# Logsumexp of a Strassen-like matmul: two row tiles by DMA transpose and last, first loads uncast, four blocks with B's sums stationary

## The chip, the cores and the metric

The kernel runs on one core of a Trainium2 chip. The metric is the device time of one execution in microseconds; lower is better. TensorE (PE) multiplies, VectorE (DVE), ScalarE (ACT) and GpSimd (POOL) do the elementwise work, GpSimd and SyncE (SP) issue the DMAs.

## The reference

```python
def setup_inputs():
    m, k, n = 1024, 4096, 4096
    return {"a": np.random.randn(m, k).astype(np.float32),
            "b": np.random.randn(k, n).astype(np.float32)}

def reference(a, b):
    x = np.matmul(a, b)
    return special.logsumexp(x, axis=-1).astype(np.float32)
```

One number per row of A: the logarithm of the sum of the exponentials of that row of A times B.

## The kernel before

Everything is multiplied in f16 and summed in f32. A has 8 row tiles of 128 rows, K has 32 tiles of 128, and B is cut into 8 column blocks of 512. A program order written by hand fixes the order of each engine.

**Stage 1, block 0.** A and B arrive by DMAs that GpSimd issues and that cast f32 to f16 on the way. A's row tiles 0 to 5 come in 8 rounds of 4 K tiles, with the matching pieces of B's block 0 between them; row tiles 6 and 7 follow in pieces of 8 K tiles. TensorE transposes each 128x128 piece of A (`transpose_group`, L194) into PSUM; VectorE and ScalarE copy it in turns to `aT`. Behind that, `plain` (L212) multiplies each transposed piece by 512 columns of block 0: 256 products of 512 columns. Six row tiles hold six PSUM banks, two banks serve the transposes; tiles 6 and 7 take banks that tiles 0 and 1 gave back. `tb` serves as staging space for the pieces of A in this stage (12 slots) and holds B's sums later.

**Blocks 1 to 7.** Each pair of row tiles (a quad q, 0 to 3), each pair of K tiles (i, 0 to 15) and the two halves of 256 columns form a 2x2 product, done with 7 products in place of 8 (a Strassen-Winograd-like scheme). It needs sums of A's parts (`s1`, `s2`, `s5` and two made in place in `aT`; `a_sums_early`, `a_sums_late`) and sums of B's parts for each block (`T1`, `T4`, `T6` in `tb`, and two made in place, called t7 and t3). `m1` to `m7` each issue 16 matmuls of 256 columns through `product` (L357), with A's side stationary (128x128, loaded anew for each matmul) and B's side moving: 7 x 16 x 4 = 448 per block. ScalarE copies parts out (`e`, `s`), VectorE puts the quad's four results together, takes each row's maximum (`lse_max`, L86), and ScalarE does the exponential with its sum (`lse_exp`, L91). In quad 3 of a block VectorE also makes the next block's sums. B's blocks are loaded one block ahead, four DMAs of 1 MB (f16) each (L130), into 8 buffers (`bt_pool`): a buffer is free once the block before has been multiplied. In block 1 the first two quads are worked on together, one quarter of K at a time.

**The end.** In the last quad of block 7 the seventh product goes to a bank of its own, `z`. While it runs, `combine` merges the maxima and sums of the eight blocks per row, and the last row tile's two halves are merged apart. Then one small DMA stores the result.

Of the kernel before, what the change touches and what calls it, by code (L numbers as in the profile page):

```python
# [13 lines left out]
def kernel(  # L14
# [21 lines left out]
    SC = 1024  # L36
    KC, JT = K // SC, SC // P
    G = 4
    GI = KP // G
    assert (MT, KT, NB) == (8, 32, 8) and JT == 2 * GI and KC == G  # L40

    a_m = a.rearrange("(p mt) k -> mt p k", mt=MT)

    cst_pool = ctx.enter_context(tc.tile_pool(name="cst", bufs=1))
    bt_pool = ctx.enter_context(tc.tile_pool(name="btp", bufs=2 * G))
    fix_pool = ctx.enter_context(tc.tile_pool(name="fix", bufs=1))
    psum_pool = ctx.enter_context(
# [20 lines left out]
    T1, T4, T6 = tb[:, 0], tb[:, 1], tb[:, 2]  # L68
    stg_slots = tb.rearrange("p t (i j) n -> p (t i) (j n)", j=4)
    NSLOT = 3 * KP // 4  # L70
    ident = cst_pool.tile([P, P], f16, name="ident")
# [40 lines left out]
    def combine(m0, m1, n, ln=True, between=None):  # L112
        nm, dd = nmmin[:, m0:m1], d[:, m0:m1, 0:n]
        nc.vector.tensor_reduce(out=nm, in_=negmax[:, m0:m1, 0:n], axis=AX.X, op=ALU.min)
        sub(dd, negmax[:, m0:m1, 0:n], nm.unsqueeze(-1).broadcast_to((P, m1 - m0, n)))
        nc.scalar.activation(out=dd, in_=dd, func=AF.Exp, scale=-1.0)
        if between:
            between()
        nc.vector.tensor_mul(out=dd, in0=dd, in1=tsum[:, m0:m1, 0:n])
        nc.vector.tensor_reduce(out=lg[:, m0:m1], in_=dd, axis=AX.X, op=ALU.add)  # L120
        if ln:
            nc.scalar.activation(out=lg[:, m0:m1], in_=lg[:, m0:m1], func=AF.Ln)

    def load_b(nb, g, parts=1):
        bt = bt_pool.tile([P, GI, 2, FD], f16, name=f"b_{nb}_{g}", tag="bt")
        step = 2 * GI // parts
        flat = bt.rearrange("p i t n -> p (i t) n")
        rows = b.rearrange("(k p) n -> p k n", p=P)
        for h in range(parts):
            nc.gpsimd.dma_start(  # L130
                out=flat[:, h * step : (h + 1) * step],
                in_=rows[:, g * 2 * GI + h * step : g * 2 * GI + (h + 1) * step, ts(nb, FD)],
            )
        return bt

    class Block:
        def __init__(self, nb):
            self.nb, self.raw = nb, []
# [4 lines left out]
        def rawg(self, g, kp, h):  # L143
            return self.raw[g][:, :, kp, ts(h, H)]

        def do_t1(self, g):
            add(T1[:, ts(g, GI)], self.rawg(g, 0, 0), self.rawg(g, 1, 1))

        def do_t4(self, g):
            sub(T4[:, ts(g, GI)], self.rawg(g, 1, 0), self.rawg(g, 0, 0))  # L150

        def do_t6(self, g):
            add(T6[:, ts(g, GI)], self.rawg(g, 0, 0), self.rawg(g, 0, 1))

        def do_t7(self, g):
            add(self.rawg(g, 1, 0), self.rawg(g, 1, 0), self.rawg(g, 1, 1))

        def do_t3(self, g):
            sub(self.rawg(g, 0, 1), self.rawg(g, 0, 1), self.rawg(g, 1, 1))
# [4 lines left out]
    blk0 = Block(0)  # L164
# [74 lines left out]
    rounds = []  # L239
    for kn in (4,) * 8:  # L240
        k0 = sum(rounds)
        rounds.append(kn)
        for m in range(MT - 2):
            arrivals.append((k0, kn, "a", m))
            if m < kn // 2:
# [8 lines left out]
    def behind(k0, kn, what, x):  # L254
# [6 lines left out]
        for k, m in todo:  # L261
            if m == MT - 2 and k == 0:
                acc.append(acc_tiles("l"))
            plain(acc[m // 2][m % 2], k // 2, k % 2, m)
        r = slice(k0 // 2, (k0 + kn) // 2)
        if what == "a" and x < MT - 2:
            if x >= 3 and len(in_place) >= 3:
                a_sums_late(*in_place.pop(0))
            if x % 2 == 1:
# [3 lines left out]
        if what == "a" and k0 + kn == KT and x in (4, 5):  # L273
            first_max(2 * x - 8)
            first_max(2 * x - 7)
        if what == "a" and x >= MT - 2:
            n = 2 * (k0 // JT) + x - (MT - 2)
            if n < 2:
                first_max(4 + n)
            elif in_place:  # L280
                a_sums_late(*in_place.pop(0))
# [7 lines left out]
    warm(10)  # L289
    blk = Block(1)  # L290

    def load(k0, kn, what, x):
        if what == "a":
            load_a(k0, kn, x)
            return
        if k0 % JT == 0:
            blk0.raw.append(bt_pool.tile([P, GI, 2, FD], f16, name=f"b_0_{k0}", tag="bt"))
        nc.gpsimd.dma_start(
            out=blk0.raw[k0 // JT][:, k0 % JT // 2],
            in_=b[k0 * P : (k0 + 2) * P, ts(0, FD)].rearrange("(t p) n -> p t n", p=P),  # L300
        )

    coming = list(arrivals)
    back = []
    for n, (k0, kn, what, x) in enumerate(arrivals):
        while coming and (coming[0][2] == "b" or loads[0] < count[0] + NSLOT):
            load(*coming.pop(0))
            if len(coming) == len(arrivals) - 3:
                make_identity(nc, ident)
                nc.gpsimd.memset(negmax, 3.0e38)  # L310
                nc.gpsimd.memset(tsum, 0.0)
        if not coming and not blk.raw:
            for g in range(G):
                blk.raw.append(load_b(1, g))
        if what == "a":
            transpose_group(k0, kn, x)
        if k0 < rounds[0] and x < 3:
            warm(1)
        if len(back) == min(3, 1 + n // 8):
            behind(*back.pop(0))  # L320
        back.append((k0, kn, what, x))
    while back:
        behind(*back.pop(0))

    for g in range(G):
        if g == 2:
            for m in range(MT - 2, MT):
                first_max(m)
        for f in (blk.do_t1, blk.do_t6, blk.do_t4, blk.do_t7, blk.do_t3):
            f(g)  # L330

    pending = []

# [5 lines left out]
    for nb in range(1, NB):  # L339
        nxt = None  # L340
        if nb + 1 < NB:
            nxt = Block(nb + 1)
            for g in range(G):
                nxt.raw.append(load_b(nb + 1, g))
        quads = {}
        for q in range(MP):
            if q not in quads:
                both = (0, 1) if nb == 1 and q == 0 else (q,)
                for p in both:
                    quads[p] = acc_tiles(f"{nb}_{p}")  # L350
# [4 lines left out]
            def product(c, lhs, rhs, start=False, g=None):  # L355
                for i in range(KP) if g is None else range(g * GI, (g + 1) * GI):
# [9 lines left out]
            first, tail = nb == 1 and q < 2, nxt is not None and q == MP - 1  # L366
            final = nxt is None and q == MP - 1
            if final:
                c22 = psum_pool.tile([P, FD], f32, name="c22", tag="ps")[:, 0:H]
            s = fix_pool.tile([P, 4, H], f32, name=f"s_{nb}_{q}", tag="s")  # L370
            x, e = s[:, 1::2], s[:, 0:2]
            if final:
                e = fix_pool.tile([P, 2, H], f32, name=f"e_{nb}_{q}", tag="e")
            if first and q == 1:
                e = e1

            def m1(c, p=q, **k):
                product(c, lambda i: s1[:, i, p], lambda i: T1[:, i], **k)
# [7 lines left out]
            def m6(c, p=q, **k):  # L386
                product(c, lambda i: aT[:, i, 0, p, 1], lambda i: T6[:, i], **k)
# [7 lines left out]
            def m4(c, **k):  # L395
                product(c, lambda i: aT[:, i, 1, q, 1], lambda i: T4[:, i], **k)

            if first and q == 0:
                for g in range(G):
                    for p in both:  # L400
                        u0, u1 = quads[p]
                        m1(u0[:, 0:H], p=p, start=True, g=g)
                        m5(u0[:, H:FD], p=p, g=g)
                        m2(u1[:, 0:H], p=p, start=True, g=g)
                        m6(u1[:, H:FD], p=p, g=g)
            elif not first:
                m1(c11, start=True)
                m5(c12)
            if not (first and q == 1):
                nc.scalar.copy(out=e, in_=r0.rearrange("p (h n) -> p h n", h=2))  # L410
            if not first:
# [4 lines left out]
            if first and q == 0:  # L416
                e1 = fix_pool.tile([P, 2, H], f32, name=f"e_{nb}_1", tag="e")
                nc.scalar.copy(out=e1, in_=quads[1][0].rearrange("p (h n) -> p h n", h=2))
            if tail:
                for g in range(G):  # L420
                    nxt.do_t1(g)
            add(s[:, 2], s[:, 2], e[:, 1])
            sub(s[:, 0], s[:, 2], e[:, 0])
            if final:
                z = psum_pool.tile([P, FD], f32, name="z", tag="ps")[:, 0:H]
# [7 lines left out]
                m7(z, start=True)  # L433
# [6 lines left out]
                combine(m0, m0 + 1, NB)  # L440
                lse_exp(c22, m0 + 1, nb, -1.0)
                sub(w[:, H : H + 1], n0, l0)
                lse_max(c21, m0 + 1, NB)
                add(y, y, c21)
# [6 lines left out]
                    between=lambda: add_max(w[:, 0:H], z, y, n0, w[:, H : H + 1]),  # L451
# [7 lines left out]
            if tail:  # L459
                for f in (nxt.do_t6, nxt.do_t3):  # L460
                    for g in range(G):
                        f(g)
            m7(c11)
# [3 lines left out]
            nc.scalar.copy(out=x[:, 1], in_=c21)  # L467
            sub(x, x, s[:, 0::2])
            add(c22, c22, x[:, 0])
            add(c11, c11, x[:, 1])  # L470
            rows = (r0, r1)
# [43 lines left out]
```

## Time and profile before

| | |
|---|---|
| time of 6 runs, median (lowest to highest) | 428.74 us (428.39 to 429.26) |
| the profiled execution's own time | 428.46 us |
| its span in the profile | 426.6 us |
| granted TensorE clock | 1.0 of full speed |

The page of the profile gives for each engine the busy time, its share of the span and the number of instructions; then the span in 40 slices of 10.67 us. In the rows of a timeline stand start, duration, engine, line, operation, output <- input, and in brackets how long the engine had been idle and what ended that. Matmuls are pipelined: the duration of a group reaches past the start of the next, so prices are taken from start to start. In the rows of the DMA issues stand the size of each and the time from issue to landing.

### The profile page before, as it was taken

The page shows a single profiled execution, that of the slowest core. Times are in us where ns is not written, and L with a number is a line of the kernel's source. Part 1 is how long each engine was busy: PE and PEld are TensorE (multiplying, and loading weights), DVE is VectorE, ACT ScalarE, POOL GpSimd, SP SyncE. Part 2 cuts the span into 40 slices and gives each one's busy share as a digit, 9 for nine tenths or more (in the row PEclk, how much of TensorE's full clock was granted, in tenths as well). Part 3 has the DMA queues.
Part 4 walks back from the last instruction along what each step waited for, and adds up shares of the span by engine and source line. Part 5 has one row for each costly group of instructions (what it writes and reads, how often), then busy time and mean ns, then how long its engine had stood idle before and what let it go on. Part 6 is the DMA issues. An engine that isn't in the chain of part 4 may idle for free.

```text
span 426.6 us, 8496 instructions
## 1 busy us (share of the span) xinstructions
PE 417.4 (98%) x3663; PEld 347.4 (81%) x3663; DVE 233.7 (55%) x517; ACT 112.6 (26%) x278; POOL 66.9 (16%) x108
## 2 busy tenths in 40 slices
PE   7999999999999999999999999999999999999995
PEld 3555565688888888888888888888888888888884
DVE  1556577745789325862369333863359531883235
ACT  1222235113222212222221222222222222222124
POOL 8667752100011000300003000300003000000000
PEclk9999999999999999999999999999999999999999
DMA  8999999999009900596009910398008930000000
GB/s 129 201 201 203 203 208 207 207 207 204 10 3 201 192 2 1 86 207 105 2 0 168 207 23 0 49 207 142 0 2 131 208 57 2 2 2 2 1 2 1
DMA packets 41717, 42.49 MB, mean 100 GB/s; under 512 B 1744, under 2 KB 40656, under 8 KB 41680
## 3 DMA queue, kind: packets, MB, share of 16 engines
q0 software_dynamic: 41536, 41.95, 59.8%
q8 instruction: 28, 0.46, 0.4%
q14 instruction: 9, 0.07, 0.0%
q1 hardware_dynamic: 144, 0.00, 0.0%
HBM read 83.89 MB, written 0.00 MB: 197 GB/s over the span
## 4 chain that ended last, share of the span: by engine, by line
PE 91%; DMA 3%; POOL 2%; DVE 2%; ACT 1%; issue 1%; DVEq 0%; ACTq 0%; POOLq 0%
DMA tb<-in_a_dram 3%; PE acc_1_0_3221 L357 2%; PE acc_0_0_2013 L357 2%; PE acc_1_0_1601 L357 2%; PE acc_0_0_929 L357 2%; PE acc_2_0_4421 L357 2%; PE acc_1_0_4293 L357 2%; PE acc_0_0_4165 L357 2%; PE acc_2_0_3889 L357 2%; PE acc_1_0_3761 L357 2%; PE acc_3_0_3477 L357 2%; PE acc_2_0_2809 L357 2%; PE acc_1_0_2681 L357 2%; PE acc_0_0_2553 L357 2%; PE acc_2_0_2269 L357 2%; PE acc_1_0_2141 L357 2%
## 5 line engine op out<-in xcount | busy, mean ns | idle before, releaser
L357 PEld LDWEIGHTS <-aT 128*128 128x128 f16 x1792 | 175.3, 98 | 20.3
L357 PEld LDWEIGHTS <-s_69 128*128 128x128 f16 x448 | 43.8, 98 | 5.3
L357 PEld LDWEIGHTS <-s_70 128*128 128x128 f16 x448 | 43.8, 98 | 5.1
L357 PEld LDWEIGHTS <-s_71 128*128 128x128 f16 x448 | 43.8, 98 | 5.1
L212 PEld LDWEIGHTS <-aT 128*128 128x128 f16 x256 | 22.7, 98 | 17.5 <-ACT aT L207 0.3
L194 PEld LDWEIGHTS <-tb 128*128 128x128 f16 x256 | 18.6, 98 | 17.9 <-DMA tb<-in_a_dram 5.6
L183 POOL DMA_DIRECT2D tb<-in_a_dram x56 | 30.2, 542 | 9.0 <-issue 2.6
L207 ACT COPY aT<-tps_88 128x512 f16<-128x512 f16 (+1 forms) x28 | 18.1, 648 | 48.0 <-PE tps_88 L194 48.0
L205 DVE COPY aT<-tps_87 128x512 f16<-128x512 f16 (+1 forms) x28 | 12.9, 462 | 28.8 <-PE tps_87 L194 28.8
L194 PE MATMUL tps_87<-ident,tb 128*128 128x128 f16 x128 | 11.7, 219 | 1.9 <-DMA tb<-in_a_dram 1.9
L83 DVE TENSOR_TENSOR aT<-aT 128x256 f16<-128x256 f16 (+1 forms) x50 | 13.3, 321 | 0.0
L194 PE MATMUL tps_88<-ident,tb 128*128 128x128 f16 x128 | 11.7, 219 | 1.6 <-DMA tb<-in_a_dram 1.4
L80 DVE TENSOR_TENSOR s_69<-aT 128x256 f16<-128x256 f16 (+1 forms) x25 | 8.0, 321 | 2.4 <-ACT aT L207 2.4
L80 DVE TENSOR_TENSOR s_71<-aT 128x256 f16<-128x256 f16 (+1 forms) x25 | 8.1, 322 | 0.0
L80 DVE TENSOR_TENSOR s_70<-aT 128x256 f16<-128x256 f16 (+1 forms) x25 | 8.0, 322 | 0.0
L130 POOL DMA_DIRECT2D b_0_2545<-in_b_dram x1 | 0.9, 881 | 45.4 <-PE acc_3_0_2397 L357 45.4
L130 POOL DMA_DIRECT2D b_0_3625<-in_b_dram x1 | 0.9, 881 | 45.4 <-PE acc_3_0_3477 L357 45.4
L130 POOL DMA_DIRECT2D b_0_2005<-in_b_dram x1 | 0.9, 881 | 45.4 <-PE acc_3_0_1857 L357 45.4
L130 POOL DMA_DIRECT2D b_0_3085<-in_b_dram x1 | 0.9, 881 | 45.4 <-PE acc_3_0_2937 L357 45.4
L130 POOL DMA_DIRECT2D b_0_1465<-in_b_dram x1 | 0.9, 876 | 45.0 <-PE acc_3_0_1317 L357 45.0
L285 PE MATMUL acc_1_86<-s_71 128*128 128x512 f16 x15 | 5.3, 482 | 1.2 <-DVE s_71 L288 1.2
L83 DVE TENSOR_TENSOR s_0_933<-s_0_933 128x256 f32<-128x256 f32 (+1 forms) x2 | 1.1, 559 | 6.1 <-ACT s_0_933 L467 6.1
(1012 smaller groups left out, 850.3 us busy)
## 6 DMA issues: line engine op xcount, KB each, us to landing
tb<-in_a_dram POOLq DMA_DIRECT2D x48, 128.0 KB, 5.9
tb<-in_a_dram POOLq DMA_DIRECT2D x8, 256.0 KB, 7.4
b_0_101<-in_b_dram POOLq DMA_DIRECT2D x4, 256.0 KB, 5.3
b_8_130<-in_b_dram POOLq DMA_DIRECT2D x4, 256.0 KB, 6.4
b_16_268<-in_b_dram POOLq DMA_DIRECT2D x4, 256.0 KB, 6.2
b_24_419<-in_b_dram POOLq DMA_DIRECT2D x4, 256.0 KB, 6.2
b_0_670<-in_b_dram POOLq DMA_DIRECT2D x1, 1024.0 KB, 13.6
b_1_672<-in_b_dram POOLq DMA_DIRECT2D x1, 1024.0 KB, 17.4
```

The lines of the kernel that those rows point to most:

```text
L80: nc.vector.tensor_tensor(out=o, in0=x, in1=y, op=ALU.add)
L83: nc.vector.tensor_tensor(out=o, in0=x, in1=y, op=ALU.subtract)
L130: nc.gpsimd.dma_start(out=flat[:, h * step : (h + 1) * step], in_=rows[:, g * 2 * GI + h * step : g * 2 * GI + (h + 1) * step, ts(nb, FD)],)
L183: nc.gpsimd.dma_start(out=slot, in_=a_m[m, :, k0 * P : (k0 + kn) * P])
L194: nc.tensor.matmul(pst[:, ts(j, P)], src[:, ts(j, P)], ident, is_transpose=True, start=(j == 0), stop=(j == kn - 1),)
L205: nc.vector.tensor_copy(out=dst, in_=v)
L207: nc.scalar.copy(out=dst, in_=v)
L212: nc.tensor.matmul(pt, aT[:, i, kp, m // 2, m % 2, :], blk0.raw[i // GI][:, i % GI, kp, :], start=(done[m] == 0), stop=(done[m] == KT - 1),)
L285: nc.tensor.matmul(acc[2][1], zeros[:, 0:P], zeros[:, 0:FD], start=True, stop=True)
L357: nc.tensor.matmul(c, lhs(i), rhs(i), start=(start and i == 0), stop=(i == KP - 1), skip_group_check=True,)
```

## The change

1. **Row tiles 6 and 7** are no longer loaded, transposed and multiplied in stage 1. GpSimd casts them to f16 from DRAM to DRAM (`a16`, in two halves of K, behind block 2's loads), and SyncE transposes them into `aT` with four transposing DMAs. VectorE makes their sums after quads 1 and 2 of block 2. Block 1 is done for three quads, worked on together, an eighth of K at a time, since it is loaded in eight pieces. The products of quad 3 (tiles 6, 7) with blocks 0 and 1 are two steps at the end of the program, with block 0 and block 1 loaded a second time (block 1 into `aT`'s space of quads 0 and 1) and block 0's sums kept in space of `s1`, `s2`, `s5` that is no longer needed.
2. **First loads.** The first piece of A and the first of block 0 come uncast by SyncE into f32 buffers; VectorE and ScalarE cast them. 6 warming matmuls stand ahead in place of 10.
3. **Blocks 3 to 6** (`wide_step`) are done in two halves of 128 of each 256 columns: B's side is stationary and A's side, all four quads at once, moves (512 columns). A product is then transposed: 128 columns of B on the partitions, 512 rows of A along the free axis. Sums over columns then lie across partitions: `lse_turned` turns 32x32 blocks on VectorE, takes maxima and sums per block, and `merge_turned` and `spread_turned` merge them on GpSimd into the space of the other blocks' maxima and sums.
4. **The end**: z's product is split into two halves of 128 columns, some of VectorE's work there is put in another order or on GpSimd.

```diff
+    def first(k0, kn, what, x):
+        if what == "a":
+            raw = fix_pool.tile([P, FD], f32, name="raw_a", tag="e")
+            ...
+            nc.sync.dma_start(out=raw, in_=a_m[x, :, k0 * P : (k0 + kn) * P])
+            nc.vector.tensor_copy(out=slot, in_=raw)
+        else:
+            raw = fix_pool.tile([P, 2, FD], f32, name="raw_b", tag="s")
+            nc.sync.dma_start(out=raw, in_=b_rows[:, 0, :, 0:FD])
+            nc.vector.tensor_copy(out=blk0.raw[0][:, 0, 0], in_=raw[:, 0])
+            nc.scalar.copy(out=blk0.raw[0][:, 0, 1], in_=raw[:, 1])
...
-    for kc in range(KC):
-        for m in range(MT - 2, MT):
-            arrivals.append((kc * JT, JT, "a", m))
...
+            if not coming:
+                for lo in range(0, KP, 2):
+                    blk1.load(lo, lo + 2)
...
+    plan = [(lambda: blk1, range(MP - 1))]
+    plan += [
+        (lambda nb=nb: Block(nb, wide=nb in WIDE), range(MP)) for nb in range(2, NB)
+    ]
+    plan += [(again0, [MP - 1]), (again1, [MP - 1])]
+    WIDE = range(3, NB - 1)
...
+    def lse_turned(c, slot, h, r, by_rows=False, late=False):
+        nm = tnm[:, 1 + h, ts(r, WN // 2)]
+        v = blocks32(slot)
+        nc.vector.transpose(out=slot, in_=c)
+        nc.vector.tensor_reduce(out=nm, in_=v, axis=AX.X, op=ALU.max, negate=True)
+        if by_rows:
+            for i in range(WN // 2):
+                nc.scalar.activation(out=v[:, i], in_=v[:, i], func=AF.Exp,
+                    bias=nm[:, i : i + 1], accum_out=tts[...])
+            return lambda: None
+        add(v, v, nm.unsqueeze(-1).broadcast_to((P, WN // 2, 32)))
+        exp = lambda: nc.scalar.activation(out=slot, in_=slot, func=AF.Exp)
+        total = lambda: nc.vector.tensor_reduce(out=tts[...], in_=v, axis=AX.X, op=ALU.add)
+        ...
+    def wide_step(blk, nxt):
+        for nt in range(2):
+            ...
+            product(c11, lambda i: blk.T1[:, i], lambda i: s1[:, i], start=True)
+            product(c12, lambda i: cols(i, 1, 1), lambda i: s5[:, i], start=True)
+            product(c21, lambda i: cols(i, 0, 0), lambda i: s2[:, i], start=True)
+            ...
+            nc.scalar.copy(out=s[:, 1], in_=c12)
+            ...
+            add(s[:, 1], s[:, 1], c21)
+            sub(s[:, 0], s[:, 1], c11)
+            ... mk("t1")
+            product(c22, lambda i: blk.T6[:, i], lambda i: aT[:, i, 0, :, 1], start=True, stop=True)
+            ... mk("t6"), mk("t3")
+            product(c12, lambda i: cols(i, 0, 1), lambda i: aT[:, i, 0, :, 0], stop=True)
+            sub(s[:, 0], c12, s[:, 0])
+            add(c22, c22, s[:, 0])
+            end12 = lse_turned(c12, slots[0], 1, 0)
+            end22 = lse_turned(c22, slots[1], 1, 1, True)
+            product(c21, lambda i: blk.T4[:, i], lambda i: aT[:, i, 1, :, 1], stop=True)
+            sub(s[:, 1], c21, s[:, 1])
+            end12()
+            end21 = lse_turned(c21, c22, 0, 1)
+            ... mk("t4"), mk("t7")
+            product(c11, lambda i: cols(i, 1, 0), lambda i: aT[:, i, 1, :, 0], stop=True)
+            add(c11, c11, s[:, 1])
+            exp11, end11 = lse_turned(c11, c12, 0, 0, late=True)
...
+                if step == 1:
+                    nxt.load(0, GI)
+                    nxt.load(GI, 2 * GI)
+                    nc.gpsimd.tensor_copy(
+                        out=ident[0:1, 0:2], in_=aT[0:1, 0, 0, MP - 1, :, 0]
+                    )
+                    nxt.load(2 * GI, 3 * GI)
+                    nxt.load(3 * GI, KP)
...
+            for h in range(2):
+                a16 = dram_pool.tile([2, P, KH], f16, name=f"a16_{h}")
+                for m in range(2):
+                    nc.gpsimd.dma_start(out=a16[m], in_=a_m[MT - 2 + m, :, ts(h, KH)])
+                for m in range(2):
+                    nc.sync.dma_start_transpose(
+                        aT[:, ts(h, KP // 2), :, MP - 1, m, :].rearrange("p i t c -> p (i t) c"),
+                        a16[m],
+                    )
...
+            if step == 1 and q == 1:
+                a_sums_early(slice(0, KP // 2), MP - 1)
+                a_sums_late(slice(0, KP // 2), MP - 1)
```

In the rows below, a row is an engine's instruction with its line, output and input, as the program orders them.

GpSimd's queue after the last pieces of A for block 0, before (`b_0_670` and on are block 1, `b_0_921` and on block 2, `b_0_1465` block 3):

```order
L183 DMA tb<-in_a_dram 128x512 x4
L183 DMA tb<-in_a_dram 128x1024 x8
L130 DMA b_0_670<-in_b_dram 128x8x512
L130 DMA b_1_672<-in_b_dram 128x8x512
L130 DMA b_2_674<-in_b_dram 128x8x512
L130 DMA b_3_676<-in_b_dram 128x8x512
L130 DMA b_0_921<-in_b_dram 128x8x512
```

And after the change (`b_0_89` and on are block 1, `b_0_747` block 2, `b_0_1204` block 3; `a_0_755` is the first half of `a16`):

```order
L210 DMA tb<-in_a_dram 128x512 x4
L154 DMA b_0_89<-in_b_dram 128x4x512 x2
L154 DMA b_3_92<-in_b_dram 128x4x512 x2
L154 DMA b_0_747<-in_b_dram 128x8x512
L154 DMA b_3_750<-in_b_dram 128x8x512
L541 DMA a_0_755<-in_a_dram 128x2048 x2
L541 DMA a_1_760<-in_a_dram 128x2048 x2
L154 DMA b_0_1204<-in_b_dram 128x8x512
L154 DMA b_1_1205<-in_b_dram 128x8x512
L529 COPY ident<-aT 1x2
L154 DMA b_2_1206<-in_b_dram 128x8x512
```

The eight pieces of tiles 6 and 7 no longer stand ahead of block 1; their copies stand behind block 2, and the second half of block 3 waits behind a small copy that reads a transposed tile.

VectorE in a block before, for one quad of block 6 (a quad is 12.2 us of TensorE's products):

```order
L80 TENSOR_TENSOR s_0_3635<-s_0_3635 128x256
L83 TENSOR_TENSOR s_0_3635<-s_0_3635 128x256
L83 TENSOR_TENSOR s_0_3635<-s_0_3635 128x2x256
L80 TENSOR_TENSOR acc_0_1_3634<-acc_0_1_3634,s_0_3635 128x256
L80 TENSOR_TENSOR acc_0_0_3633<-acc_0_0_3633,s_0_3635 128x256
L86 TENSOR_REDUCE negmax<-acc_0_0_3633 128x1
L86 TENSOR_REDUCE negmax<-acc_0_1_3634 128x1
```

And in the first half of block 3 after the change, from the fifth product's end to the sums of the next half (`wide_0_0` to `wide_0_3` are c11, c12, c21, c22; `ident` holds the maxima, `tb` the two slots and the sums):

```order
L89 TENSOR_TENSOR sw_0_1775<-wide_0_1_1772,sw_0_1775 128x512
L86 TENSOR_TENSOR wide_0_3_1774<-wide_0_3_1774,sw_0_1775 128x512
L383 STREAM_TRANSPOSE tb<-wide_0_1_1772 128x512
L384 TENSOR_REDUCE ident<-tb 128x16
L86 TENSOR_TENSOR tb<-tb,ident 128x512
L383 STREAM_TRANSPOSE tb<-wide_0_3_1774 128x512
L384 TENSOR_REDUCE ident<-tb 128x16
L89 TENSOR_TENSOR sw_0_1775<-wide_0_2_1773,sw_0_1775 128x512
L397 TENSOR_REDUCE tts<-tb 128x16
L383 STREAM_TRANSPOSE wide_0_3_1774<-wide_0_2_1773 128x512
L384 TENSOR_REDUCE ident<-wide_0_3_1774 128x16
L86 TENSOR_TENSOR wide_0_3_1774<-wide_0_3_1774,ident 128x512
```

Per 512 rows and 256 columns of the result, the maximum was taken in place on PSUM; now a block transpose, a maximum, a subtraction and a sum over 512 elements stand for each of the four parts (for c22 only the first two).

More of the change, by code (lines that the diff above doesn't have):

```diff
@@ L122, in combine, with __init__, load @@
             nc.scalar.activation(out=lg[:, m0:m1], in_=lg[:, m0:m1], func=AF.Ln)
[L124 to L129, printed above, removed]
+    b_rows = b.rearrange("(i t p) n -> p i t n", p=P, t=2)
+    class Block:
+        def __init__(self, nb, raw=None, sums=None, wide=False):
+            self.nb = nb
+            self.wide = wide
+            self.raw = raw or [
+                bt_pool.tile([P, GI, 2, FD], f16, name=f"b_{nb}_{g}", tag="bt")
+                for g in range(G)
+            ]
+            self.T1, self.T4, self.T6 = sums or (tb[:, 0], tb[:, 1], tb[:, 2])
+            if wide:
+                self.T1, self.T4, self.T6 = [
+                    t[:, 0 : KP // 2].rearrange("p i (j n) -> p (i j) n", j=2)
+                    for t in (self.T1, self.T4, self.T6)
+                ]
+        def load(self, lo, hi):
@@ L353, with product @@
             c21, c22 = r1[:, 0:H], r1[:, H:FD]
[L355 to L356 removed]
+            def product(c, lhs, rhs, start=False, k=(0, KP)):
+                for i in range(*k):
                     nc.tensor.matmul(
```

444 lines of the change are left out of this document (312 added, 132 removed).

## The prediction

> **What bounds the kernel now.** I read the busy shares of the page first, then TensorE's waits, then the timeline at the start, at the seam between block 0 and block 1, and at the end.
>
> ```profile
> PE 417.4 (98%) x3663; PEld 347.4 (81%) x3663; DVE 233.7 (55%) x517; ACT 112.6 (26%) x278; POOL 66.9 (16%) x108
> PEclk9999999999999999999999999999999999999999
> GB/s 129 201 201 203 203 208 207 207 207 204 10 3 201 192 2 1 86 207 105 2 0 168 207 23 0 49 207 142 0 2 131 208 57 2 2 2 2 1 2 1
> ...
> PE tps_87 L194 <- DMA tb<-in_a_dram: 1.9, 3, 0.9
> PE tps_88 L194 <- DMA tb<-in_a_dram: 1.4, 1, 1.4
> PE acc_1_86 L285 <- DVE s_71 L288: 1.2, 1, 1.2
> ```
>
> TensorE is busy 98% of the span at full granted clock, and all its named waits are 4.5 us, at the start. So only fewer or shorter products, an earlier start or a shorter end can help, and any new wait of TensorE costs its full length. Loads run at 201 to 208 GB/s while they run, and they run without a gap for the first ten slices (107 us): there the loads are nearly as tight as TensorE.
>
> ```profile
> 59.33 0.61 PE L194 MATMUL tps_87<-ident,tb 128*128 128x128 f16 x8
> 60.64 0.61 PE L194 MATMUL tps_88<-ident,tb 128*128 128x128 f16 x8
> 61.95 0.61 PE L194 MATMUL tps_87<-ident,tb 128*128 128x128 f16 x8
> 62.40 1.03 PE L212 MATMUL acc_1_86<-b_24_419,aT 128*128 128x512 f16 x4
> 63.26 0.61 PE L194 MATMUL tps_88<-ident,tb 128*128 128x128 f16 x8
> 72.71 1.89 PE L212 MATMUL acc_l_781<-b_16_268,aT 128*128 128x512 f16 x8
> 79.62 0.60 PE L357 MATMUL acc_0_0_929<-tb,s_69 128*128 128x256 f16 x4
> 421.53 0.60 PE L357 MATMUL z<-b_3_3631,aT 128*128 128x256 f16 x4
> ```
>
> Two unit prices follow. From 72.71 to 79.62 stand 32 plain products of 512 columns: 6.91/32 = 215.9 ns each. From 79.62 to the last four products at 421.53 stand 3132 products of 256 columns: 341.91/3132 = 109.2 ns each. Two of the narrow ones cost 218.4 ns, 2.5 ns more than one wide one. Eight transposes take 62.40 - 61.95 = 0.45 us, 56 ns each.
>
> **The change, part by part.**
>
> *Row tiles 6 and 7 leave stage 1.* Row tile 5, the last of the six, ends its plain products at 63.26. From there to 79.62 TensorE only does the transposes and plain products of tiles 6 and 7: 16.36 us. Three more groups of their transposes lie ahead of 63.26 (at 59.33, 60.64, 61.95), 3 x 0.45 = 1.35 us. Both go: -17.7 us. Block 0 of these tiles comes back at the end as 7 x 16 = 112 narrow products, 112 x 109.2 ns = +12.2 us. Block 1's fourth quad only moves: 0. Net -5.5 us.
>
> *First loads by SyncE.* At the start:
>
> ```profile
> 0.86 0.27 DVE L288 MEMSET s_71<- 128x256 uint32 x1 [0.86 <-PEq L499]
> 1.24 0.68 POOL L183 DMA_DIRECT2D tb<-in_a_dram  x1 [0.80 <-POOLq L499]
> 1.91 0.72 POOL L298 DMA_DIRECT2D b_0_101<-in_b_dram  x1
> 4.64 0.39 PE L194 MATMUL tps_87<-ident,tb 128*128 128x128 f16 x4
> 9.08 0.40 PE L194 MATMUL tps_87<-ident,tb 128*128 128x128 f16 x4 [0.52 <-DMA tb<-in_a_dram]
> ```
>
> GpSimd's queue loses two issues (0.68 + 0.72 us), so the third piece of A, which TensorE takes at 9.08, can come 1.4 us sooner. It gains nothing if the transfers themselves set that time. At most the first transposes come 2 us sooner: SyncE starts about when VectorE does (0.86) and needs a landing and a cast. I take -1.4 us, since the issues stand one behind the other, and keep 0 and -2. The new end of block 0's six tiles, T, is then 63.26 - 1.35 - 1.4 = 60.5 us.
>
> *Blocks 3 to 6 with B stationary.* 4 x 448 narrow products become 4 x 224 wide ones: 896 x 215.9 - 1792 x 109.2 ns = 193.4 - 195.7 = -2.2 us. The moving operand is now sometimes four strided runs of 128, which no row shows; bounds: 0 (a wide one costs two narrow ones) and -2.2.
>
> This gain is free only if VectorE keeps up. Each half block gives it 20 operations on 512 f32 and 20 sums on 512 f16, and the time of a half block on TensorE is 112 x 215.9 ns = 24.2 us.
>
> ```profile
> 411.48 0.42 DVE L80 TENSOR_TENSOR acc_2_0_4421<-acc_2_0_4421,s_2_4423 128x256 f32<-128x256 f32 x1
> 411.94 0.69 DVE L86 TENSOR_REDUCE negmax<-acc_2_0_4421 128x1 f32<-128x512 f32 x1
> 412.55 0.68 DVE L86 TENSOR_REDUCE negmax<-acc_2_1_4422 128x1 f32<-128x512 f32 x1
> ...
> 12.25 0.28 DVE L80 TENSOR_TENSOR s_69<-aT 128x256 f16<-128x256 f16 x1
> 12.45 0.28 DVE L80 TENSOR_TENSOR s_70<-aT 128x256 f16<-128x256 f16 x1
> ...
> 119.70 0.68 DVE L80 TENSOR_TENSOR tb<-b_0_921 128x1024 f16<-128x1024 f16 x1
> 120.30 0.68 DVE L80 TENSOR_TENSOR tb<-b_1_923 128x1024 f16<-128x1024 f16 x1
> ```
>
> A 512-wide f32 operation has its successor 0.61 us later (411.94 to 412.55) if independent, and 0.69 + 0.04 = 0.73 us later if it must end first (as 411.48 to 411.94 is 0.42 + 0.04). F16 sums follow each other after 0.20 us (256) and 0.60 us (1024), so about 0.33 for 512, at most 0.42. A half block costs VectorE 20 x 0.61 + 20 x 0.33 = 18.8 us at best, 20 x 0.73 + 20 x 0.42 = 23.0 us at worst, under 24.2: it hides. Four of the 20 are block transposes, which this trace doesn't have; I price them as the reductions of the same size. ScalarE gets 16 small exponentials with an accumulator read each besides five larger instructions:
>
> ```profile
> 421.36 0.20 ACT L122 ACTIVATE lg<-lg 128x1 f32<-128x1 f32 x1 [0.43 <-DVE lg L120]
> ...
> 421.83 0.19 ACT L91 ACTIVATION_READ_ACCUMULATOR c_4551<-c_4551,negmax 128x1 f32 x1
> ```
>
> The exponential here is narrower (1 column, not 32), so 0.20 is a lower bound; with its read 16 x 0.4 = 6.4 us, and five larger ones of at most 0.7: some 10 us of 24.2, hidden even at twice that price for the small ones (16). GpSimd's merges of 96 columns have a half block to themselves.
>
> *Transposing DMAs.* The loads must come first. With them at about 205 GB/s, block 2's last piece ended in the old order here:
>
> ```profile
> 80.08 0.88 POOL L130 DMA_DIRECT2D b_3_927<-in_b_dram x1 [2.58 <-PE acc_l_782 L212]
> ...
> b_3_927<-in_b_dram POOLq DMA_DIRECT2D x1, 1024.0 KB, 28.4
> out_dram<-lg SPq DMA_DIRECT2D x1, 4.0 KB, 1.4
> ```
>
> 80.1 + 28.4 = 108.5 us. The stream now has 2.1 MB of tiles 6 and 7 less ahead of it (10.2 us) and starts about 1.4 us sooner: 97 us. The f16 copies of tiles 6 and 7 follow, 2.1 MB, to 107; the first half stands at 102. The transposed tiles are wanted by VectorE's five sums (about 3.3 us) ahead of quad 3 of block 2, which starts at T + 336 x 0.1092 + 3 x 12.23 = 133.9 us: they must land by 130. That is 28 us for four transposing DMAs, 7 us each. As an ordinary load each (0.52 MB at 205 GB/s) takes 2.6 us. If its sixteen 128x128 blocks went one behind another, each with the 1.4 us that the small store needs from issue to landing, it would take 22 us. I take twice the load, 5 us, nearer to the load, because loads of a thousand rows show no such series (1 MB took 5.1 us). No stall then. VectorE's order carries the wait: were the tiles late, sums of block 3 and every bank's release behind them would be late too.
>
> No row here shows a transposing DMA. The Trainium skill ("DMA: Bandwidth & Descriptors", Latency and other measured facts) gives 261 GB/s with a non-contiguous middle dimension, 2.0 us for each of the four: by it the sum stays. "VectorE: DVE Perf Modes" (The three transpose paths) lists 1309 ns for one 128x128 on the DMA path; if that added up over 64 blocks it would be 84 us, about 55 us past the limit. That speaks against this change, and no run here shows which holds.
>
> *Block 1 on the heels of its load.* T1 and T6 of each eighth arrive 2.6 us apart (0.52 MB); the 24 products of an eighth take 24 x 0.1092 = 2.62 us. Blocks 1 and 2 (8.4 MB) take the stream's last 41 us before 97, so the first eighth lands at 97 - 41 + 2.6 = 58.6, 1.9 us before T; two sums of 0.35 leave about 1 us in hand. At the seam to block 2, T1's last quarter waits for the last correction of quad 2 (0.69 + 2 x 0.43 us of VectorE) and can hold TensorE 0.3 us. I put +0.5 us for such seams.
>
> *The end.*
>
> ```profile
> 422.01 0.41 DVE L80 TENSOR_TENSOR e_3_4553<-e_3_4553,acc_3_1_4550 128x256 f32<-128x256 f32 x1
> 422.61 0.48 DVE L101 CUSTOM_DVE_ANT_0 s_3_4552<-z,e_3_4553,s_3_4552 128x256 f32<-128x256 f32 x1
> ```
>
> The last products end at about 421.53 + 0.60 = 422.1, and VectorE takes them at 422.61, busy with other work until then. With that work moved ahead or to GpSimd and half of z taken earlier, about 0.5 us is saved; two halves of z cost 32 x 56 - 16 x 109 ns = +0.05.
>
> *Sum:* -17.7 + 12.2 - 1.4 - 2.2 + 0.5 - 0.5 = -9.1 us. The profiled execution took 428.46 us (span 426.6): 419.4. The runs' median is 0.28 above that execution: **419.7 us**.
>
> **The rivals.**
>
> *A. The transposing DMAs are late* (slower than before). Every microsecond past 130 us falls on TensorE at quad 3 of block 2. For: no row shows one, and the upper bound is 22 us each. Against: loads of the same bytes need 2.6. At 10 us each they end at 142, 12 us late: 432. It turns slower from (28 + 9)/4 = 9.3 us each; at 22 us, 60 us late, 480. At 7 to 9 us each it ends between 420 and 428. The second rule above would be this rival at its upper end.
>
> *B. VectorE becomes the bound in blocks 3 to 6.* For: 23.0 of 24.2 us in the worst pricing. If a block transpose took 1.4 us, twice a reduction, the half block would be 23.0 + 2.8 = 25.8, 1.6 over, times 8 = 13 us: 433; with the best pricing, 18.8 + 2.8, nothing. Against: the work is spread and the two ends average 20.9. Likely price if it comes: 2 to 6 us, 422 to 426.
>
> *C. The start gives nothing and block 1 is held by its loads.* Eight smaller pieces at 2.8 instead of 2.6 us give 8 x 0.2 = 1.6 us; with the 1.4 us of the start, 422.7. For: the slices at 201 to 208 GB/s have no slack. Against: each eighth has about 1 us in hand.
>
> *D. The wide products gain nothing* (four strided runs): +2.2, 421.9; inside the forecast's own range.
>
> **How the numbers follow.** The forecast (with D in it) has 0.67, its own range 417.5 to 422. C has 0.12 (422 to 424), B 0.10 (422 to 434, 0.03 of it slower), A 0.11 (0.06 of it slower). The range 416.8 to 425.5 leaves out the upper parts of A and B (about 0.13) and a little below (0.05). Within 0.2% (428 to 429.6) counts as no change that a measurement could tell. Slower: 0.06 + 0.03 = 0.09; same 0.02; faster 0.89.
>
> **What would show it.** Right: wide products at 216 ns with no wait of TensorE inside blocks 3 to 6; block 1's first products at about 60.5 us; the transposing DMAs landed before 130 us; VectorE 80 to 95% busy in blocks 3 to 6; the last product near 413 us. Wrong: a wait of TensorE on VectorE's sums of quad 3 at about 134 us (A), on T4 or T1 at a half block's seam (B), or on the pieces of block 1 between 60 and 82 us (C).

## The result, and the profile after

| | before | after |
|---|---|---|
| median (lowest to highest), us | 429.03 (428.39 to 430.63), 20 runs | 419.89 (419.5 to 420.5), 10 runs |
| the profiled execution's own time, us | 428.46 | 419.58 |
| its span, us | 426.6 | 417.8 |

The ratio is 0.9786, 95% interval [0.9776, 0.9796]: 9.1 us faster. The forecast was 419.7.

First the page of the changed kernel (busy times, granted clock), then its waits of TensorE (in total, times, longest):

```profile
PE 410.9 (98%) x2763; PEld 260.8 (62%) x2763; DVE 316.0 (76%) x709; ACT 120.6 (29%) x447; POOL 100.3 (24%) x191
PEclk9999999999999999999999999999999999999999
...
PE acc_1_98 L300 <- DVE s_73 L303: 1.2, 1, 1.2
PE tps_99 L221 <- DMA tb<-in_a_dram: 0.9, 3, 0.4
PE acc_1_94 L239 <- ACT aT L234: 0.2, 1, 0.2
PE acc_0_93 L239 <- DVE aT L232: 0.2, 1, 0.2
PE tps_99 L221 <- DVE tb L314: 0.2, 1, 0.2
```

TensorE still sets the time: 98% busy at full clock, 2.7 us of named waits in place of 4.7, all of them in stage 1. VectorE went from 55% to 76%. The timeline of TensorE (start, duration) at the places that the sum rests on:

```profile
4.13 0.61 PE L221 MATMUL tps_99<-ident,tb 128*128 128x128 f16 x4 [0.20 <-DVE tb L314]
8.98 0.39 PE L221 MATMUL tps_99<-ident,tb 128*128 128x128 f16 x4
61.02 0.38 PE L565 MATMUL acc_0_0_765<-tb,s_71 128*128 128x256 f16 x2
97.76 1.91 PE L565 MATMUL acc_0_0_1215<-tb,s_71 128*128 128x256 f16 x16
134.51 1.91 PE L565 MATMUL acc_3_0_1615<-tb,s_71 128*128 128x256 f16 x16
146.74 3.62 PE L450 MATMUL wide_0_0_1771<-s_71,tb 128*128 128x512 f16 x16
340.13 1.91 PE L565 MATMUL acc_0_0_3263<-tb,s_71 128*128 128x256 f16 x16
412.63 1.06 PE L565 MATMUL z_4067<-aT 128*128 128x128 f16 x16
```

Block 1 begins at 61.02 (T; 60.5 was forecast). From 61.02 to 97.76 stand block 1's 336 products, 36.74/336 = 109.3 ns each, so they never waited for their loads. Quad 3 of block 2 begins at 134.51, where 36.74 + 336 x 0.1092 us behind T put it (134.45): tiles 6 and 7 were there in time. From 146.74 to 340.13 stand the 896 wide products, 193.39/896 = 215.8 ns each. The last product ends at 412.63 + 16 x 0.056 = 413.5.

The span divides into three pieces:

| piece | before | after | difference | forecast |
|---|---|---|---|---|
| stage 1, to T | 79.62 | 61.02 | -18.6 | -17.7 - 1.4 = -19.1 |
| T to the last product's end | 421.97 - 79.62 = 342.35 | 413.53 - 61.02 = 352.51 | +10.2 | 12.2 - 2.2 + 0.5 = +10.5 |
| the rest of the span | 4.63 | 4.27 | -0.4 | -0.5 |

They sum to -8.8, as the spans do (417.8 - 426.6).

SyncE's part of the timeline of the changed kernel, then VectorE's and GpSimd's rows that wait for it:

```profile
100.12 20.95 SPq L543 DMA_TRANSPOSE aT<-a_0_755  x2
121.11 4.64 SPq L543 DMA_TRANSPOSE aT<-a_1_760  x2
...
132.29 0.69 DVE L86 TENSOR_TENSOR s_71<-aT 128x1024 f16<-128x1024 f16 x1 [1.53 <-DMA aT<-a_1_760]
...
123.96 0.18 POOL L529 COPY ident<-aT 1x2 f16<-1x2 f16 x1 [25.26 <-DMA aT<-a_0_755]
```

The first two transposing DMAs held SyncE for 21 us, the other two for 4.6. The last landed at about 132.3, when VectorE, which had waited 1.53 us, went on. The four took 32 us from 100.1, 8 us each, more than the 7 that the prediction allowed; yet TensorE didn't wait. The second half of `s_71` was done at 132.98 and is read by the ninth product of the quad, at 134.51 + 8 x 0.109 = 135.4: 2.4 us in hand.

Last, the busy time of each engine in three wide half blocks of the changed kernel (the first, the second and the last; columns PE, PEld, DVE, ACT, POOL, granted clock, DMA share, GB/s):

```profile
146.74:170.91 24.17, 24.17 (x114) 10.94 (x112) 16.29 (x36) 4.28 (x17) 2.66 (x4) 1.00 1.07 175
170.91:195.09 24.18, 24.18 (x114) 10.98 (x112) 20.17 (x42) 7.43 (x38) 3.10 (x7) 1.00 0.00 1
315.97:340.10 24.13, 24.13 (x113) 10.94 (x112) 23.26 (x42) 7.41 (x38) 4.71 (x8) 1.00 0.02 2
```

VectorE is busy 20.2 of 24.2 us in a half block in the middle, but 23.3 in the last one, where it makes block 7's sums, 1024 wide.

### The profile page after: what moved, and what is told of

Read it like the earlier page. It is cut to its first block, busy times and chain, and to the rows that moved or that the text cites. A ratio compares the mean times of both kernels' runs of the same rounds, so it can differ in the third digit from the quotient of the medians.

```text
span 417.8 us, 7137 instructions
## 1 busy us (share of the span) xinstructions
PE 410.9 (98%) x2763; PEld 260.8 (62%) x2763; DVE 316.0 (76%) x709; ACT 120.6 (29%) x447; POOL 100.3 (24%) x191
## 4 chain that ended last, share of the span: by engine, by line
PE 91%; DMA 6%; DVE 1%; issue 1%; POOL 1%; ACT 0%; POOLq 0%; DVEq 0%
DMA tb<-in_a_dram 5%; PE acc_1_0_1347 L565 2%; PE acc_1_0_767 L565 2%; PE acc_1_0_3395 L565 2%; PE acc_2_0_769 L565 2%; PE acc_3_0_3851 L565 2%; PE acc_3_0_1615 L565 2%; PE acc_0_0_1215 L565 2%; PE acc_3_0_3715 L565 2%; PE acc_2_0_3579 L565 2%; PE acc_0_0_3263 L565 2%; PE acc_2_0_1482 L565 2%; PE acc_0_0_765 L565 2%; PE wide_1_2_3078 L450 2%; PE wide_1_0_2700 L450 2%; PE wide_0_1_2517 L450 2%
## 5 line engine op out<-in xcount | busy, mean ns | idle before, releaser
L565 PEld LDWEIGHTS <-aT 128*128 128x128 f16 x848 | 81.7, 98 | 9.4
L450 PEld LDWEIGHTS <-tb 128*128 128x128 f16 x384 | 37.6, 98 | 45.1
L387 ACT ACTIVATE tb<-tb,ident 128x32 f32<-128x32 f32 x128 | 39.1, 306 | 6.4 <-DVE ident L384 6.4
L408 POOL TENSOR_TENSOR ident<-ident,tmin 128x96 f32<-128x96 f32 x8 | 3.1, 386 | 134.9 <-DVE tmin L410 134.9
L396 ACT ACTIVATE tb<-tb 128x512 f32<-128x512 f32 x8 | 5.0, 630 | 90.1 <-DVE tb L86 90.1
L210 POOL DMA_DIRECT2D tb<-in_a_dram x47 | 25.6, 547 | 6.4 <-issue 1.5
L239 PEld LDWEIGHTS <-aT 128*128 128x128 f16 x192 | 16.6, 98 | 13.9 <-DVE aT L232 1.4
L234 ACT COPY aT<-tps_100 128x512 f16<-128x512 f16 x24 | 14.1, 586 | 38.7 <-PE tps_100 L221 38.7
L232 DVE COPY aT<-tps_99 128x512 f16<-128x512 f16 x24 | 10.2, 424 | 19.7 <-PE tps_99 L221 19.7
L387 ACT ACTIVATION_READ_ACCUMULATOR tb<-tb,ident 128x1 f32 x128 | 23.8, 186 | 0.0
L221 PEld LDWEIGHTS <-tb 128*128 128x128 f16 x192 | 14.5, 99 | 14.1 <-DMA tb<-in_a_dram 2.8
L565 PEld LDWEIGHTS <-s_71 128*128 128x128 f16 x208 | 20.4, 98 | 2.8
L565 PEld LDWEIGHTS <-s_73 128*128 128x128 f16 x208 | 20.3, 98 | 2.4
L565 PEld LDWEIGHTS <-s_72 128*128 128x128 f16 x208 | 20.3, 98 | 2.4
L384 DVE TENSOR_REDUCE ident<-tb 128x16 f32<-128x512 f32 x16 | 11.0, 687 | 1.1
```

Source lines behind the costliest of these rows:

```text
L210: nc.gpsimd.dma_start(out=slot, in_=a_m[m, :, k0 * P : (k0 + kn) * P])
L221: nc.tensor.matmul(pst[:, ts(j, P)], src[:, ts(j, P)], ident, is_transpose=True, start=(j == 0), stop=(j == kn - 1),)
L232: nc.vector.tensor_copy(out=dst, in_=v)
L234: nc.scalar.copy(out=dst, in_=v)
L239: nc.tensor.matmul(pt, aT[:, i, kp, m // 2, m % 2, :], blk0.raw[i // GI][:, i % GI, kp, :], start=(done[m] == 0), stop=(done[m] == KT - 1),)
L384: nc.vector.tensor_reduce(out=nm, in_=v, axis=AX.X, op=ALU.max, negate=True)
```

## Experiments

### The parts one by one

`no_wide` leaves blocks 3 to 6 narrow, and leaves the merging of the turned sums out:

```diff
-    WIDE = range(3, NB - 1)
+    WIDE = range(0)
```

> Blocks 3 to 6 are done like block 2 (A stationary, 256 columns moving) and the merging of turned maxima is left out with them; everything else is as in the changed kernel. Theory (the wide form saves only the 2.5 ns per pair of products): 1792 x 109.2 - 896 x 215.9 ns = 2.2 us more, 422.1 us. Rival (the wide form also saves or costs something at its seams or in the merging): more than 1 us away from 422.1.

Measured: 422.42 us (ratio to before 0.9843, 95% interval [0.983, 0.9856]), 2.5 us more than after.

`no_sync` gives the first loads back to GpSimd, which casts them:

```diff
-        if len(coming) >= len(arrivals) - 2:
+        if False:
             first(k0, kn, what, x)
```

> The first piece of A and the first of block 0 come by GpSimd with the cast again; the rest is the changed kernel, 6 warming matmuls included. Theory (the two issues that leave GpSimd's queue bring the stream forward): T, the start of block 1's products, moves from 61.0 to about 62.0 us and the time to 420.8. Rival (the transfers set the pace from the first piece on): T and time stay within 0.3 us.

Measured: 420.82 us (0.9808 [0.9796, 0.9821]), 0.9 us more.

`rows_alone` has both edits; of the change, the move of tiles 6 and 7 and the new order of the end are left.

> Only the move of row tiles 6 and 7 (and the new order of the end) is left of the change: first loads by GpSimd, blocks 3 to 6 narrow, the merging of turned sums left out. If the three parts add up (wide products 2.5 us, first loads 0.9 us, as undone one by one), 419.9 + 3.4 = 423.3 us; my own terms gave 428.7 - 5.5 + 0.5 - 0.5 = 423.2. Rival: the parts lean on one another (the earlier start also brings the loads of block 1 sooner, the narrow blocks hide more at their seams): then it is off 423.3 by more than 0.5.

Measured: 422.70 us (0.9853 [0.9836, 0.987]): 6.3 us faster than before [5.6, 7.0]. Both edits together cost 2.8 us, 0.6 less than the 3.4 that they cost one by one, so the rival's bar of 0.5 was just passed. The timelines of TensorE tell where that lies: the first product of block 1 and the first of `z`, in `no_wide`, `no_sync` and `rows_alone`.

```profile
61.29 0.38 PE L565 MATMUL acc<-tb,s 128*128 128x256 f16 x2
414.25 1.95 PE L565 MATMUL z<-aT 128*128 128x128 f16 x32
```

```profile
62.64 0.38 PE L565 MATMUL acc<-tb,s 128*128 128x256 f16 x2
413.37 1.95 PE L565 MATMUL z<-aT 128*128 128x128 f16 x32
```

```profile
62.18 0.38 PE L565 MATMUL acc<-tb,s 128*128 128x256 f16 x2
415.14 1.95 PE L565 MATMUL z<-aT 128*128 128x128 f16 x32
```

From T to `z` it is 352.96 us in `no_wide` and 352.96 in `rows_alone`, both with narrow blocks; 350.73 in `no_sync`, with wide ones. In after, `z` starts at 411.74, 350.72 behind T. The wide products are worth 2.23 us, to a hundredth the same with either start: this part adds up. The start does not repeat so well. T was 62.64 and 62.18 in the two kernels where GpSimd does the first loads, and between 60.49 and 61.29 (mean 60.87) in the eight profiles where SyncE does. That is 1.5 us by the profiles, 0.9 by the timed runs. Behind `z`, `no_wide` takes 0.4 us longer to its end than the other two. So by the profiles the miss lies at the two ends of the program. T alone differs by up to 0.8 us between the eight profiles, so the 0.6 may be scatter; no run shows that it is.

### The transposing DMAs and the loads beside them

After's GpSimd issues half of block 3's loads at 96.91 and 97.80, and holds the other half back by a copy that reads a transposed tile. `no_hold` takes that copy out:

```diff
                     nxt.load(GI, 2 * GI)
-                    nc.gpsimd.tensor_copy(
-                        out=ident[0:1, 0:2], in_=aT[0:1, 0, 0, MP - 1, :, 0]
-                    )
                     nxt.load(2 * GI, 3 * GI)
```

> GpSimd's small copy that holds block 3's second half back until row tiles 6 and 7 are transposed is taken out, so all four loads of block 3 stand in the queues beside the transposing DMAs. Theory (loads in flight slow the transposing DMAs): in the changed kernel the two issued beside block 3's first loads kept SyncE 9 and 12 us each and the two issued after those loads 2.3 us each; now all four take about 10 us each, the last lands near 100 + 40 + 8 = 148 in place of 132, and VectorE's sums for quad 3 come about 13 us after TensorE wants them: 419.9 + 13 = 433 us, with that wait of TensorE at about 135 us. Rival (the first two are slow because the casting copies of tiles 6 and 7 are still running, or because a transposing DMA has a slow start): the last still lands near 132 and the time stays at 419.9, within 1 us.

`hold_all` puts the copy ahead of all four loads:

```diff
-                    nxt.load(0, GI)
-                    nxt.load(GI, 2 * GI)
                     nc.gpsimd.tensor_copy(
                         out=ident[0:1, 0:2], in_=aT[0:1, 0, 0, MP - 1, :, 0]
                     )
+                    nxt.load(0, GI)
+                    nxt.load(GI, 2 * GI)
```

> The same small copy is put ahead of all four loads of block 3, so no load stands beside the first two transposing DMAs except the last casting copies. Theory (loads slow them): all four are issued at about 2.3 us each, tiles 6 and 7 stand before 120 us, TensorE never waits there, and the time stays at 419.9, within 1 us, since the transposed tiles were in time already; block 3's loads start 15 to 20 us later than the first ones did and end near 135 to 140, about when VectorE wants them. Rival (copies or a slow start): the first pair again keeps SyncE 20 us and the last lands near 132.

Measured: `no_hold` 427.89 us (0.9974 [0.9964, 0.9984]), `hold_all` 419.50 (0.9781 [0.9767, 0.9795]). SyncE's timeline and one tile's instructions (duration ns: lowest/median/highest) of `no_hold`, then VectorE's first sums of tiles 6 and 7, and TensorE from the last product of quad 2 of block 2 (138.65) to the third of quad 3:

```profile
99.54 37.57 SPq L540 DMA_TRANSPOSE aT<-a  x4
...
L540 SPq DMA_TRANSPOSE aT<-a x4: 2170/10643/13976, 99.5 to 134.9; - x4
DMA to landing us min/median/max: 4.5/17.6/25.5
...
134.70 1.90 DVE L86 TENSOR_TENSOR s<-aT 128x1024 f16<-128x1024 f16 x3 [10.75 <-DMA aT<-a]
...
138.65 3.57 PE L562 MATMUL acc<-b,aT 128*128 128x256 f16 x16 [5.88 <-ACT s L715]
142.02 2.72 PE L562 MATMUL acc<-tb,s 128*128 128x256 f16 x16
144.58 3.66 PE L562 MATMUL acc<-b,s 128*128 128x256 f16 x32
```

The same views of `hold_all`:

```profile
99.58 14.65 SPq L543 DMA_TRANSPOSE aT<-a  x4
...
L543 SPq DMA_TRANSPOSE aT<-a x4: 1787/2938/6853, 99.6 to 112.5; - x4
DMA to landing us min/median/max: 4.9/6.1/10.0
```

The same four DMAs hold SyncE for 37.6 us beside all of block 3's loads (4 MB in f16), for 25.6 (20.95 + 4.64) beside half of them, in after, and for 14.7 with none of them. In `hold_all` the first two take 9.4 us of that, against 21 in after; so neither a slow start nor the casting copies ahead of them account for the 21.

In `no_hold` the second DMA, issued at 109.1, landed 25.5 us later. VectorE's sums of the first half, which stand between quads 1 and 2, waited 10.75 us for it. VectorE and ScalarE work in program order, so ScalarE's copy (L715) for quad 2 came late, and TensorE waited 5.88 us for it, at quad 2's last product and not at quad 3. Its next two groups of 16 products, started 3.37 and 2.56 us ahead of the group behind them instead of 1.75, lose 2.4 us more: 8.3, against 8.0 measured. The forecast's rival A is a real mechanism, though it strikes one product earlier than the forecast had it; the copy of two elements keeps it away. My 433 was too high, since I priced the fourth DMA like the others and put the wait behind it: it began at 134.9, with the loads over, took 2.2 us, and VectorE waited only 0.92 us for its tile. `hold_all` has VectorE's 1.5 us wait away as well, and its time can't be told from after's: from T to `z` it is 350.73 us there too (60.70 to 411.43).

### VectorE's room in blocks 3 to 6

`dve5` adds five reductions, whose result nobody reads, to VectorE's work in every half block; `dve12` adds twelve. They stand ahead of the correction of `c12`:

```diff
             product(c12, lambda i: cols(i, 0, 1), lambda i: aT[:, i, 0, :, 0], stop=True)
+            for _ in range(5):
+                nc.vector.tensor_reduce(
+                    out=extra, in_=blocks32(s[:, 0]), axis=AX.X, op=ALU.max
+                )
             sub(s[:, 0], c12, s[:, 0])
```

> In each of the eight half blocks of blocks 3 to 6 VectorE does 5 more reductions of 512 f32 elements (about 0.61 us each, into a scratch tile that nobody reads), ahead of the correction that follows the fifth product: 3.0 us more per half block. Theory (VectorE has idle time of 24.17 - 20.2 = about 4 us per half block in the changed kernel): nothing, 419.9 within 1 us. Rival (VectorE already bounds these blocks, or its lag reaches TensorE at once): 8 x 3.0 = 24 us more, 444.

> The same with 12 more reductions, 7.3 us per half block. Theory: 20.2 + 7.3 - 24.2 = 3.3 us too much per half block; TensorE can run some 5 us ahead before it needs the part sum that VectorE takes from c21, so 8 x 3.3 - 5 = 21 us more, 441 us, with TensorE waiting for VectorE at each half block but the first one or two. Rival (VectorE's work there hangs on nothing TensorE waits for): 420.

Measured: `dve5` 425.51 us (0.9926 [0.9909, 0.9942]), `dve12` 466.98 (1.0887 [1.087, 1.0903]). Neither theory had `dve5` right, and the 441 for `dve12` was 26 us too low. The waits of TensorE in `dve12`, and its timeline at three of them (L570 and L451 are after's L565 and L450):

```profile
PE wide L451 <- ACT sw L468: 23.8, 7, 5.0
PE acc L570 <- ACT s L637: 10.3, 1, 10.3
...
303.77 5.30 PE L451 MATMUL wide<-aT,b 128*128 128x512 f16 x16 [2.12 <-ACT sw L468]
308.91 3.62 PE L451 MATMUL wide<-aT,tb 128*128 128x512 f16 x16
...
333.13 3.61 PE L451 MATMUL wide<-aT,b 128*128 128x512 f16 x16 [3.34 <-ACT sw L468]
336.58 3.62 PE L451 MATMUL wide<-aT,tb 128*128 128x512 f16 x16
...
362.49 5.17 PE L451 MATMUL wide<-aT,b 128*128 128x512 f16 x16 [5.03 <-ACT sw L468]
367.49 3.62 PE L451 MATMUL wide<-aT,tb 128*128 128x512 f16 x16
```

In `dve12` VectorE sets the time of every half block but the first. The seven waits inside half blocks are 23.8 us, near the 21 of the theory; it left out the wait at the seam to block 7, 10.3 us, and slow products behind the waits. The 16 products behind a wait take 3.45 us to the next group when they aren't slow. Behind two of the eight waits, of 1.46 and 3.34 us, they took just that; behind the other six TensorE lost 1.5 to 2.9 us each, 11.6 in all. With the 34.1 us of waits that is 45.7 of the 47.1 us. In `dve5`, VectorE's row of the five and TensorE's only wait in blocks 3 to 7:

```profile
335.36 3.55 DVE L489 TENSOR_REDUCE extra<-sw 128x16 f32<-128x512 f32 x5
...
349.53 0.69 DVE L87 TENSOR_TENSOR wide<-wide,sw 128x512 f32<-128x512 f32 x1
...
350.94 3.05 PE L570 MATMUL acc<-b,aT 128*128 128x256 f16 x16 [4.18 <-ACT s L637]
353.79 2.47 PE L570 MATMUL acc<-tb,aT 128*128 128x256 f16 x16
356.10 1.91 PE L570 MATMUL acc<-b,aT 128*128 128x256 f16 x16
```

No half block waits; the loss stands at the seam to block 7. ScalarE's copy into the single buffer `s` must wait until VectorE has added `c11` from it (L87, here at 349.53), and block 7's fifth product (`m3`, at 350.94) waits for the copy. To see whether the lag of seven half blocks or the last one's own load pays for it, `dve5_but_last` has the five in all but the last, `dve5_last` in the last alone:

```diff
-            for _ in range(5):
+            for _ in range(0 if last else 5):
```

```diff
-            for _ in range(5):
+            for _ in range(5 if last else 0):
```

> The five extra reductions in every half block of blocks 3 to 6 but the last. Seam theory: each half block lags only 0.14 us behind, 1.0 us over seven, less than the 1.8 us in hand at the copy that block 7 needs: no wait of TensorE, 419.9 to 420.4. Rival, VectorE's shortage is paid inside the half blocks: 423 or more.

> The five extra reductions in the last half block alone. Seam theory: 3.6 us more of work against 1.8 us in hand, a wait of TensorE of 1.8 to 3.2 us at block 7's third product and some slower products after it: 422 to 424.5. Rival: 419.9, as one half block of eight can't pay more than an eighth of 5.6 us (420.6 at most).

Measured: 421.15 us (0.9811 [0.9797, 0.9826]) and 421.36 (0.982 [0.9804, 0.9836]). VectorE's addition and TensorE's wait at the seam, in after (where nothing waits), in `dve5_but_last` and in `dve5_last`:

```profile
343.94 0.69 DVE L86 TENSOR_TENSOR wide_1_0_3076<-wide_1_0_3076,sw_1_3080 128x512 f32<-128x512 f32 x1
...
347.12 0.60 PE L565 MATMUL acc_0_0_3263<-b_0_2884,aT 128*128 128x256 f16 x4
```

```profile
346.14 0.69 DVE L87 TENSOR_TENSOR wide<-wide,sw 128x512 f32<-128x512 f32 x1
...
347.56 1.91 PE L570 MATMUL acc<-b,aT 128*128 128x256 f16 x16 [0.61 <-ACT s L637]
```

```profile
346.92 0.69 DVE L87 TENSOR_TENSOR wide<-wide,sw 128x512 f32<-128x512 f32 x1
...
348.34 1.91 PE L570 MATMUL acc<-b,aT 128*128 128x256 f16 x16 [1.20 <-ACT s L637]
```

Where TensorE waits, it starts 1.42 us after the addition. In after that would be 345.36, and it started at 347.12: 1.76 us in hand. Against T (61.02, 60.68, 60.88, and 60.49 in `dve5`, in this order), the addition is 2.5 us late in `dve5_but_last`, 3.1 in `dve5_last`, 6.1 in `dve5`. Less the 1.76 that makes 0.8, 1.4 and 4.4 us, and TensorE's rows stand 0.8, 1.4 and 4.35 us late. So both rivals of the two expectations fall, but my numbers missed as well: the seven half blocks lag 2.5 us and not 1.0, and the last one brings its 3.1 and no slow products, so 421.4 and not 422 to 424.5. The times of the two exceed after's by 1.3 and 1.5 us, of `dve5` by 5.6: the two lags have one reserve to use up, and a wait of 4.2 us brings slow products (2.85 and 2.31 us to the next group in place of 1.75, +1.7 us), which a wait of 1.2 didn't.

## Why the prediction was right, step by step

- **What bounds the kernel.** Right: products removed from TensorE are time removed. Its named waits were 4.7 us, not 4.5 (a fourth row had 0.2); nothing hangs on that.
- **Tiles 6 and 7 out of stage 1, -17.7 + 12.2.** Right. Alone with the new end it brought 6.3 us [5.6, 7.0]. The terms for it, -5.5 + 0.5 - 0.5, give 5.5, just outside; with the seams and the end as measured (0.1 and 0.4, below) they give 5.8.
- **Seams of block 1, +0.5.** Wrong: the piece from T to the last product is 352.51 us, and products alone make 342.35 + 12.23 - 2.24 + 0.05 = 352.39. The seams cost 0.1.
- **First loads by SyncE, -1.4.** Inside the bounds of 0 and -2. The profiles of before and after show -0.9 (T at 61.02 against 63.26 - 1.35 = 61.91), as the timed runs do; the profiles of all kernels show -1.5. Which is nearer stays open. The step that was priced is there: GpSimd issues the third piece of A at 3.26 in place of 4.62, 1.4 us sooner. TensorE's row at 8.98, only 0.1 sooner than before, can't show what that brought: it waits for no DMA there, and has by then done eight products of block 0, where before had done four. `no_sync`, with after's order, has this row at 10.45, 1.5 us later. But there TensorE is also slow for longer: its second group of four transposes takes 0.63 us (0.39 in after). No run parts the two.
- **Wide products, -2.2.** Right: 2.23 us, 215.8 ns each, four strided runs or not. Rival D is out.
- **VectorE keeps up.** Right, and rival B didn't come. The block transposes take 0.71 to 0.73 us against the reductions' 0.69, as they were priced. But the working took all half blocks alike at 18.8 to 23.0 us: the last has 23.3, and the room is 1.76 us at the seam behind it.
- **Transposing DMAs, 5 us each, limit 7.** The outcome was right and both numbers wrong: they took 8 us each, and the limit was 8.6: the sum of the second half must start 0.69 us ahead of 135.4, at 134.7, and (134.7 - 100.1)/4 = 8.6. I had wanted both halves at the quad's start. The step left out the loads of block 3, which the order printed ahead of the prediction shows in GpSimd's queue beside them. That no wait came was in part luck: with all of block 3's loads beside them it did come, in `no_hold`, and nothing in the prediction priced the copy that holds half of them back. An estimate by the 261 GB/s of the Trainium skill ("DMA: Bandwidth & Descriptors", Latency and other measured facts) is 2.0 us each: the two behind the loads held SyncE for 2.25 and 2.34 us, near it, those beside the loads for 9.3 and 11.6, far from it. Its other figure ("VectorE: DVE Perf Modes", The three transpose paths), 1309 ns for one 128x128, would add up to 21 us each, again an estimate, and isn't borne out where block 3's loads are held: 1.8 to 6.9 us in `hold_all`.
- **The end, -0.5.** The rest of the span shrank by 0.4; no run undoes the new end alone, so it isn't shown that the new order did it.
- **Rival C** (block 1 held by its loads): no; 336 products at 109.3 ns.

The terms that missed, +0.5 and -1.4, missed in opposite directions by 0.4 and 0.5: the 0.2 us between forecast and result is better than its terms.

## What to carry to other kernels

Price a transfer together with what the other queues have in flight at that time, and if it must be early, hold the others back: here one copy of two elements is worth 8 us. Read an engine's room in its worst stage, not in the mean: VectorE had 4 us per half block and 1.8 at the seam behind the last. Small lags in several places add up silently until one reserve is used up, and only then cost time.

## What the runs showed of the hardware

Transposing DMAs suffer beside ordinary loads: one of 0.5 MB held SyncE for 1.8 to 6.9 us with no load of block 3 in flight (the 6.9 beside the last casting copies), and up to 14.0 beside them, with 4.9 to 10.0 us to its landing without them and up to 25.5 with them.

TensorE can be slow after a wait, and the length of the wait alone doesn't tell whether. Behind waits of 4.18 us (`dve5`) and 5.88 us (`no_hold`) the next products lost 1.7 and 2.4 us. In `dve12` two waits of 5.03 us cost about 1.6 each and one of 2.12 us 1.7, while of two waits of 3.34 us one cost 2.9 and the other nothing. Waits of 0.61, 1.20 and 1.46 us cost nothing. The granted clock goes with it: 0.67 over the 16 products behind the 2.12 us (303.77 to 308.91), 1.00 behind the 3.34 us that cost nothing (333.13 to 336.58). The Trainium skill ("TensorE: Matmul & The Clock Gate", Part 1: The HAM clock gate) says that the array falls to half its clock after an idle window of about 3.4 us, and needs about as long under load to come back. An estimate by the page, 3.4 us at half clock, loses 1.7 us, near most of these rows. Read as the length of a wait, the 3.4 us doesn't hold here, and the measurement decides: 2.12 us was enough once.

The clock of `dve12` suggests why. It falls to half at 215.48, 246.20, 273.51, 304.23, 362.25 and 386.15 us, and these six times lie whole multiples of 3.41 us apart (9, 8, 9, 17 and 7 of them). On that grid the wait of 2.12 us (301.65 to 303.77) lies whole between two points, 300.81 and 304.23, and the 3.34 us that cost nothing (329.79 to 333.13) are cut by the point at 331.53 into 1.7 and 1.6. So where a wait falls seems to count beside its length; this is read from one trace, and no run tested it.
